# K to gates in a Griffin-style layer: K's second half in another tile order, the first gates' raw weights loaded once, their sums in a pool of their own

## The chip, the cores and the metric

The kernel runs on one core of one Trainium2 chip, in one launch. The metric is the device time of that core in microseconds (us). A time is the median of several executions; beside it stands one profiled execution with its own time.

TensorE (PE) multiplies matrices, VectorE (DVE), ScalarE (ACT) and GpSimd (POOL) work elementwise, SyncE (SP) issues DMAs only. ScalarE issues DMAs too. Each engine runs its own list of instructions in order and waits at semaphores for the others.

## The reference

One layer of a streaming encoder over 1024 tokens, with 1024 channels and 16 heads of 64, in float32:

```python
h = rmsnorm(x, ln1_g[l]) * (1.0 + sc1) + sh1
p = h @ w_in[l]
q, k, v, cb, cc, cx, ga, gb = jnp.split(p, split_at, axis=-1)
q = rmsnorm(q.reshape(b, s_len, SB_HEADS, SB_HEAD_DIM), q_norm_g[l])
k = rmsnorm(k.reshape(b, s_len, SB_HEADS, SB_HEAD_DIM), k_norm_g[l])
v = v.reshape(b, s_len, SB_HEADS, SB_HEAD_DIM)
y_a = stick_breaking_attention(q, k, v)
y_b = cb * causal_dwconv(cc * cx, conv_w[l])
merged = (jax.nn.sigmoid(ga) * (y_a @ w_branch_a[l])
          + jax.nn.sigmoid(gb) * (y_b @ w_branch_b[l]))
x = x + g1 * (merged @ w_out[l])

h = rmsnorm(x, ln2_g[l]) * (1.0 + sc2) + sh2
f = (jax.nn.silu(h @ w_ffn_gate[l]) * (h @ w_ffn_up[l])) @ w_ffn_down[l]
x = x + g2 * f
```

Here the change touches how `k`, and then `q`, `cb`, `cc`, `cx`, `ga` and `gb` are computed.

## The kernel before

**Numbers.** Every product is computed from two parts of each float32 operand, a rounded one (hi) and the rest (lo), as three matmuls: hi·hi, lo·hi and hi·lo. ScalarE makes hi with a copy, VectorE makes lo by a subtraction. A pair hi/lo made from weights is `whi` and `wlo`; `hh[n]` and `hl[n]` (shown as `big`) hold the parts of h, transposed, for token half n and eight chunks of channels.

**Stages.** Normalisation of x; V; K; the "gates" (the other six column sections of `w_in`); attention; branches and output; the FFN. The change is where K ends and the gates begin, at some 100 to 215 us.

**K.** Two column halves (`cc` = 1, 2, loop at L450), each over eight tiles of 128 tokens. A tile is a product of 24 matmuls (`mm_tok`, L308) into a bank `pj`, and then `finish_k` (L395): ScalarE squares (`qsq`, L397), VectorE adds up per head (`qss`, L399), POOL makes the reciprocal root in two steps (`rs_m`, L122, and `rs_r`, L123), VectorE scales (`qn`, L402). What stands behind the `yield`, TensorE's transposes (`tr`, L408), hi and lo (`khl`, L411 on ScalarE and L412 on VectorE) and the two stores to `d_k` (L414, issued by ScalarE), is run two tiles later, from the list `tails`; the last two are run between the first products of the gates. Beside K, a generator (`ml`, `more()`) makes sums of parts of h, which are written to `d_t` on SyncE (L376) and come back as the factors of the gates.

**Gates.** 20 gates of 1024 x 256 weight columns (1024 x 1024 per section, in four): four of q, eight of the convolution, eight of the gates proper. Each gate is a 2 x 2 block product with seven products in place of eight (Winograd's form): p1 to p7, each 12 matmuls (`half_prod`, L131 to L133). The raw weights of a gate are two 512 KB loads (`g_raw`, L478, a ring of two buffers): a11 and a12 in the first, a21 and a22 in the second. POOL makes s3 = a11 − a21, s2 = a22 − s3, s1 = a21 + a22 and s4 = a12 − s2 (`ws`, L136 and L653). `g_split` (L489) splits each, p1 and p2 take the first raw half as it is. The other factor is a part of h (p1, p2, p3) or one of the sums `d_t`: `ft5` with s2 (p6), `ft4` with s1 (p5), `ft6` with s3 (p7), and d_t3 with a22 (p4), which is loaded into `hh[1][:, 0:4]` and `hl[1][:, 0:4]` (L644; K's last tiles read these before). Products are combined into `c` on VectorE; the first `c` is a copy of p1 on ScalarE (L682).

The products p1 and p2 of gates 0 and 1 run ahead (`pre`, L505 to L516), straight behind K, from a raw half each; for their other products both gates load both raw halves (again).

**q.** Each finished quarter of q goes through `put_q`: hi and lo (`gt`, L588 on ScalarE, L589 on VectorE) are stored to `d_q`, then its square (`c`, L590) is split into hi (`gt`, L591) and lo (`gt`, L136, the helper of all VectorE and POOL operations on two tensors), and `sum_q` (L599) adds the squares up with a one-hot matmul `tr<-gt,sel`, some products later (`later`).

**Order.** What runs when on each engine is decided by a scheduler that places instructions by their dependences and expected times, in the order of the program where these don't decide; `tc.high_priority()` moves what is inside ahead of what competes with it, `tc.issue_after` holds something behind a given instruction. Names that end in a number are buffers or versions of a tile.

Of the kernel before, what the change touches and what calls it, by code (L numbers as in the profile page):

```python
# [29 lines left out]
def block_kernel(tc, x, x_t, cols, ada_1, ada_2, ada_row, w_q, w_kv, w_v1, w_cg, w_a, w_b, w_o, w_g, w_u, w_d, out):  # L30
# [8 lines left out]
    def nm(s):  # L39
        uid[0] += 1  # L40
        return f"{s}_{uid[0]}"
# [100 lines left out]
    def ps_pj():  # L142
        return pps.tile([P, 512], F32, tag="pj", bufs=6, name=nm("pj"))
# [301 lines left out]
    def more():  # L445

        with tc.issue_after(ends[0]), tc.issue_after(ends[1]):
            next(ml, None)

    for cc in (1, 2):  # L450
        w = wq[4:] if cc == 1 else [load_w(w_kv[cc, j]) for j in range(4)]
        for i in range(8):
            ps = ps_pj()
            mm_tok(ps, i, w, 0, 8)
            while len(tails) >= 2:
                next(tails.pop(0), None)
            tails.append(finish_k(ps, i, cc - 1))
            next(tails[-1])
            for _ in range(2 if (cc, i) < (1, 4) else 3):
                more()  # L460
            if (cc, i) == (2, 1):
                for _ in ml:
                    pass
                s2b.close()
                sx.close()

    ftx = ExitStack()
    ftp = ftx.enter_context(tc.tile_pool(name="phft", bufs=1, side="right", reuse_waits="tile"))
    ft = {q: ftp.tile([P, 2, 4, 512], F32R, name=f"ft{q}") for q in (5, 4)}
    for q in (5, 4):  # L470
        nc.sync.dma_start(ft[q].bitcast(F32), d_t[q])

    def g_bank():
        return ps_pj()

    def g_raw(src):
        raw = gw.tile([P, 1024], F32, tag="raw", bufs=GR, name=nm("raw"))
        last_raw[0] = nc.sync.dma_start(raw, src)  # L478
        return raw
# [5 lines left out]
    def g_split(src):  # L485
# [4 lines left out]
        tt(nc.vector, lo, src, hi.bitcast(F32), ALU.subtract)  # L490
        return hi, lo

    fac = {0: (hh[0][:, 0:4], hl[0][:, 0:4]), 1: (hh[0][:, 4:8], hl[0][:, 4:8]), 2: (hh[1][:, 4:8], hl[1][:, 4:8])}
    def g_prod(w, q):
        ps = g_bank()
        half_prod(ps, w, *fac[q])
        return ps

    gates = ([(5, j) for j in range(4)] + [(sec, j) for j in range(4) for sec in (1, 2)] +
             [(sec, j) for sec in (4, 3) for j in range(4)])  # L500

    def w_of(sec, m):
        return w_q[m] if sec == 5 else w_cg[sec, m]

    pre = {}  # L505

    def first_two(g):
        sec, j = gates[g]
        raw = g_raw(w_of(sec, j))
        return g_prod(g_split(raw[:, :512]), 0), g_prod(g_split(raw[:, 512:]), 1)  # L510

    for g in range(NG):
        pre[g] = first_two(g)
        if g == 0:
            for tl in tails:
                next(tl, None)  # L516

    def two_raw(g):
        sec, j = gates[g]
        return g_raw(w_of(sec, j)), g_raw(w_of(sec, j + 4))  # L520

    s2.close()
    sw.close()
# [3 lines left out]
    gp = sg_.enter_context(tc.tile_pool(name="phg1", bufs=1, reuse_waits="tile"))  # L527

    split_at.append(gp)
    ft[6] = gp.tile([P, 2, 4, 512], F32R, name="ft6")  # L530
    for q, t in ft.items():
        fac[q] = (t[:, 0], t[:, 1])
    fac[3] = (hh[1][:, 0:4], hl[1][:, 0:4])
# [103 lines left out]
        nc.scalar.dma_start(d_y[m, :, s:s + 512], y)  # L637

    uc = {}
    raws = two_raw(0)  # L640
    pend, pmm, eq = [], [], end_q()
    nc.sync.dma_start(ft[6].bitcast(F32), d_t[6])
    for e in range(2):
        nc.sync.dma_start(fac[3][e].bitcast(F32), d_t[3][:, e])  # L644
    for g, (sec, j) in enumerate(gates):
        raw, raw2 = raws
        p1, p2 = pre[g] if g in pre else (g_prod(g_split(raw[:, :512]), 0), g_prod(g_split(raw[:, 512:]), 1))
        a11, a12, a21, a22 = raw[:, :512], raw[:, 512:], raw2[:, :512], raw2[:, 512:]
        s1, s2_, s3, s4 = (gp.tile([P, 512], F32, tag=f"ws{q}", bufs=1, name=nm("ws")) for q in range(4))
        tt(nc.gpsimd, s3, a11, a21, ALU.subtract)  # L650
        tt(nc.gpsimd, s2_, a22, s3, ALU.subtract)
        tt(nc.gpsimd, s1, a21, a22, ALU.add)
        ws4 = nc.gpsimd.tensor_tensor(out=s4, in0=a12, in1=s2_, op=ALU.subtract)  # L653
        if g + 1 < len(gates):
            raws = two_raw(g + 1)
        c11, c21, c12, c22 = (gp.tile([P, 512], F32, tag=f"c{q}", bufs=2, name=nm("c")) for q in range(4))

        def put(c, m, n):
            if sec == 5:
                pend.append((c, m, n))  # L660
            elif sec > 2:
                nc.scalar.activation(c, c, AF.Sigmoid)
                nc.scalar.dma_start((d_sga, d_sgb)[sec - 3][m, :, n * 512:(n + 1) * 512], c)
            elif sec == 1:
                ccs[m, n] = c
            elif n == 1 and m >= 4:
                ccs["late"] = c
            else:
                put_u(c, m, n)
                if n == 0 and m >= 4:  # L670
                    put_u(ccs["late"], m, 1)

        def later():
            if len(pmm) > 1 or pmm and not pend:
                sum_q(*pmm.pop(0))
            if pend:
                put_q(*pend.pop(0))
            elif g > 3 and not pmm:
# [24 lines left out]
        put(c21, j + 4, 0)  # L703
        if g + 1 == len(gates):
            for _ in eq:
                pass
        for _ in range((5 if sec in (3, 4) else 0) if g + 1 < len(gates) else 50):
            next(ml, None)
    sg_.close()
    ftx.close()  # L710
    split_at[:] = [gw]
# [887 lines left out]
```

## Time and profile before

| | us |
|---|---|
| median of 3 executions | 1842.04 (1841.74 to 1842.79) |
| profiled execution, its own time | 1840.08 |
| its span | 1838.3 |
| mean granted clock of TensorE | 0.998 |

The span is what the page and the views divide; the execution's own time lies 1.8 us above it. Rows of a timeline give start, duration, engine and line, operation, output and inputs (partitions x elements) and, in brackets, how long the engine had been idle and what ended that. A row with x2 or x3 is several in sequence. "SPq" and "ACTq" are DMAs issued by SyncE or ScalarE. TensorE is continuously busy from 66 to 178 us, and the stretch of the change ends at some 215.

### The profile page before, as it was taken

To read this page: it belongs to the slowest core of one execution; us is meant where nothing else is said; L and a number is where in the kernel's file an instruction comes from. 1 tells how busy PE (TensorE), PEld (TensorE's weight loads), DVE (VectorE), ACT (ScalarE), POOL (GpSimd) and SP (SyncE) were. 2 spreads that over 40 slices of the span, in tenths; PEclk is the share of its full clock that TensorE was granted. 3 is DMA by queue.
4 is the path that set the end of the run, shared out by engine and by line. 5 is a ranking of instruction groups with operands and counts; after the bars stand their busy time and mean duration, and the time that the engine had idled before them with its cause. 6 is when DMAs were issued, how large, how long until landed. Compare 5 with 4: busy or idle time off the path is not lost.

```text
span 1838.3 us, 24895 instructions
## 1 busy us (share of the span) xinstructions
PE 1803.6 (98%) x8829; PEld 1501.9 (82%) x8829; DVE 1353.5 (74%) x1949; ACT 792.3 (43%) x1494; POOL 366.4 (20%) x277
## 2 busy tenths in 40 slices
PE   7999999999999999999999999999999999999999
PEld 4787778888889988888888788877888888878887
DVE  7873776779874888888887644589877788644776
ACT  3452553333343656665665311664444344422321
POOL 0043327423240000000000000105544454200000
PEclk9999999999999999999999999999999999999999
DMA  9598452217748566588544636424533344299766
GB/s 395 198 317 303 162 188 76 86 70 260 275 157 265 153 183 180 178 240 278 153 133 141 209 126 209 142 92 161 195 138 147 130 172 170 103 340 334 283 228 221
DMA packets 147267, 358.01 MB, mean 195 GB/s; under 512 B 15480, under 2 KB 44480, under 8 KB 144968
## 3 DMA queue, kind: packets, MB, share of 16 engines
q1 hardware_dynamic: 101816, 289.12, 46.3%
q10 hardware_dynamic: 44320, 63.64, 9.9%
q0 software_dynamic: 1008, 3.67, 0.5%
q8 instruction: 70, 1.15, 0.3%
q14 instruction: 53, 0.43, 0.1%
HBM read 245.74 MB, written 110.66 MB: 194 GB/s over the span
## 4 chain that ended last, share of the span: by engine, by line
PE 76%; DVE 11%; DMA 6%; issue 3%; ACT 3%; POOL 0%; ACTq 0%; SPq 0%; DVEq 0%; POOLq 0%
PE e L131 6%; PE e L132 6%; PE e L133 6%; PE pj L131 5%; PE pj L133 5%; PE pj L132 5%; PE pj L308 5%; PE pj L892 4%; PE pj L893 4%; PE pj L894 4%; PE e L1427 4%; PE e L1426 4%; PE e L1428 4%; PE tr L819 3%; PE o L835 2%
## 5 line engine op out<-in xcount | busy, mean ns | idle before, releaser
L804 DVE TENSOR_TENSOR_SCAN pt<-pt,mk 128x128 f32<-128x128 f32 (+7 forms) x128 | 172.1, 1350 | 48.8 <-ACT pt L800 48.6
L800 ACT ACTIVATE pt<-z,rq 128x512 f32<-128x512 f32 (+3 forms) x192 | 107.3, 580 | 88.9 <-PE z L799 57.4
L131 PE MATMUL e<-big,whi 128*128 128x512 f32 x352 | 137.7, 391 | 1.9 <-ACT c L1326 1.9
L133 PE MATMUL e<-big,wlo 128*128 128x512 f32 x352 | 137.7, 391 | 0.0
L132 PE MATMUL e<-big,whi 128*128 128x512 f32 x352 | 137.6, 391 | 0.0
L136 DVE TENSOR_TENSOR c<-e,c 128x512 f32<-128x512 f32 x138 | 93.0, 687 | 56.0 <-PE e L133 55.0
L122 POOL TENSOR_SCALAR rs_m<-ss 128x1 f32<-128x1 f32 x8 | 1.5, 192 | 651.8 <-ACT xn L1229 651.8
L131 PE MATMUL pj<-big,whi 128*128 128x512 f32 x320 | 125.1, 391 | 0.5 <-DVE c L136 0.4
L132 PE MATMUL pj<-big,whi 128*128 128x512 f32 x320 | 124.7, 390 | 0.0
L133 PE MATMUL pj<-big,wlo 128*128 128x512 f32 x320 | 124.4, 390 | 0.0
L1426 PE MATMUL e<-whi,f 128*128 128x512 f32 (+1 forms) x319 | 121.7, 382 | 1.6 <-DMA f<-d_f 1.6
L1427 PE MATMUL e<-wlo,f 128*128 128x512 f32 (+1 forms) x319 | 121.8, 382 | 0.0
L1428 PE MATMUL e<-whi,f 128*128 128x512 f32 (+1 forms) x319 | 121.6, 382 | 0.0
L136 DVE TENSOR_TENSOR c<-pj,c 128x512 f32<-128x512 f32 x140 | 93.2, 682 | 27.3 <-PE pj L133 26.4
L136 DVE TENSOR_TENSOR wlo<-raw,whi 128x512 fp32r<-128x512 f32 x116 | 88.1, 763 | 34.2 <-ACT whi L489 34.1
L308 PE MATMUL pj<-whi,big 128*128 128x512 f32 x352 | 109.4, 396 | 3.7 <-ACT big L291 3.6
L489 ACT ACTIVATE whi<-raw 128x512 fp32r<-128x512 f32 x116 | 72.7, 631 | 89.1 <-PE pj L132 38.8
L823 DVE TENSOR_TENSOR atl<-tr,ath 128x512 fp32r<-128x512 f32 (+1 forms) x192 | 99.6, 548 | 14.4 <-ACT ath L822 12.6
L136 POOL TENSOR_TENSOR ws<-raw,raw 128x512 f32<-128x512 f32 x40 | 55.4, 1384 | 273.6 <-DMA raw<-w_cg 165.2
L822 ACT ACTIVATE ath<-tr 128x512 fp32r<-128x512 f32 (+1 forms) x192 | 86.9, 490 | 44.8 <-PE o L834 26.0
L132 PE MATMUL e<-rl,whi 128*128 128x512 f32 x264 | 103.6, 392 | 2.5 <-DVE rl L136 2.5
L892 PE MATMUL pj<-big,whi 128*128 128x512 f32 x256 | 103.9, 406 | 0.0
(258 smaller groups left out, 5015.9 us busy)
## 6 DMA issues: line engine op xcount, KB each, us to landing
f<-d_f SPq DMA_DIRECT2D x77, 512.0 KB, 3.6
d_f<-fs SPq DMA_DIRECT2D x70, 512.0 KB, 3.2
raw<-w_cg SPq DMA_DIRECT2D x40, 512.0 KB, 4.4
raw<-w_u SPq DMA_DIRECT2D x26, 512.0 KB, 3.2
raw<-w_g SPq DMA_DIRECT2D x25, 512.0 KB, 3.4
ad<-ada ACTq DMA_DIRECT2D x19, 512.0 KB, 5.0
ada<-ada SPq DMA_DIRECT2D x8, 1024.0 KB, 9.6
d_t<-ts SPq DMA_DIRECT2D x16, 512.0 KB, 4.0
```

Of the source, the lines that this page charges most:

```text
L131: nc.tensor.matmul(ps, wh[:, k, :], fh[:, k, :], start=(k == 0), stop=False)
L132: nc.tensor.matmul(ps, wh[:, k, :], fl[:, k, :], start=False, stop=False)
L133: nc.tensor.matmul(ps, wl[:, k, :], fh[:, k, :], start=False, stop=(k == 3))
L136: eng.tensor_tensor(out=out, in0=a, in1=b, op=op)
L308: nc.tensor.matmul(ps, a, b, start=(k == 0 and q == 0), stop=(k == KT - 1 and q == 2))
L800: nc.scalar.activation(pt[:, off + s0:off + s0 + m], z[:, :m], AF.Sigmoid, scale=rq[:, 1, i, h:h + 1])
L804: nc.vector.tensor_tensor_scan(out=pt[:, rev], data0=pt[:, rev], data1=mk[:, rev], initial=1.0, op0=ALU.mult, op1=ALU.max)
L823: nc.vector.tensor_tensor(out=tl[:, :nb, c0:c0 + P], in0=src, in1=th[:, :nb, c0:c0 + P].bitcast(F32), op=ALU.subtract)
L892: nc.tensor.matmul(ps, wh, rh_, start=(k == 0), stop=False)
L1426: nc.tensor.matmul(o, sh, w[0][:, c], start=(j == 0), stop=False)
L1427: nc.tensor.matmul(o, sh, w[1][:, c], start=False, stop=False)
L1428: nc.tensor.matmul(o, sl, w[0][:, c], start=False, stop=(j == NJ - 1))
```

## The change

- The second half of K (`cc` = 2) takes its tiles in the order 4, 5, 6, 7, 0, 1, 2, 3. After four of them, no matmul of K reads `hh[1]` any more, and d_t3 is loaded over it there.
- Gate 1's first raw half is loaded for `pre` first and split within K's loop; then both raw halves of gate 0 are loaded, and kept for all of gate 0's products. Gate 1's first half is still loaded twice. Products p1 and p2 of gate 1 now run ahead of gate 0's.
- The sums `ws` have a pool of their own (`gp2`), so that they need not wait for the pools of the K stage to be given back. For gate 0, s3, s2 and the split of s2 (`w6`) are under high priority; the split of s2 is written ahead of the other products for all gates.
- ft6 is loaded under high priority, behind the last raw load.
- For gate 0, p3 is computed ahead of p7.
- The stores of K: in both kernels all 32 are issued by ScalarE; none stands on SyncE's queue.

```diff
-    for cc in (1, 2):
-        w = wq[4:] if cc == 1 else [load_w(w_kv[cc, j]) for j in range(4)]
-        for i in range(8):
...
+    for cc in (1, 2):
+        w = wq[4:] if cc == 1 else [load_w(w_kv[cc, j]) for j in range(4)]
+        for i_, i in enumerate(range(8) if cc == 1 else (4, 5, 6, 7, 0, 1, 2, 3)):
+            if (cc, i_) == (2,4):
+                for e in range(2):
+                    ld = nc.sync.dma_start((hh, hl)[e][1][:, 0:4].bitcast(F32), d_t[3][:, e])
+            if (cc, i_) == (2,3):
+                raw1 = g_raw(w_of(*gates[1]))
+                pre_w = [(g_split(raw1[:, :512]), g_split(raw1[:, 512:]))]
+                raws = two_raw(0)
             ps = ps_pj()
             mm_tok(ps, i, w, 0, 8)
...
-    pre = {}
-
-    def first_two(g):
-        sec, j = gates[g]
-        raw = g_raw(w_of(sec, j))
-        return g_prod(g_split(raw[:, :512]), 0), g_prod(g_split(raw[:, 512:]), 1)
-
-    for g in range(NG):
-        pre[g] = first_two(g)
-        if g == 0:
-            for tl in tails:
-                next(tl, None)
...
+    pre_w.append((g_split(raws[0][:, :512]), g_split(raws[0][:, 512:])))
+    pre = {1: tuple(g_prod(pre_w[0][q], q) for q in range(2))}
+    for tl in tails:
+        next(tl, None)
+    pre[0] = tuple(g_prod(pre_w[1][q], q) for q in range(2))
...
     split_at.append(gp)
+    for t_ in ("whi", "wlo"):
+        gp.tile([P, 512], F32R, tag=t_, bufs=GS2, name=nm(t_))
     ft[6] = gp.tile([P, 2, 4, 512], F32R, name="ft6")
+    sg2 = ExitStack()
+    gp2 = sg2.enter_context(tc.tile_pool(name="phg2", bufs=1, reuse_waits="tile"))
...
-    raws = two_raw(0)
     pend, pmm, eq = [], [], end_q()
-    nc.sync.dma_start(ft[6].bitcast(F32), d_t[6])
-    for e in range(2):
-        nc.sync.dma_start(fac[3][e].bitcast(F32), d_t[3][:, e])
+    with tc.high_priority(), tc.issue_after(last_raw[0].ins):
+        nc.sync.dma_start(ft[6].bitcast(F32), d_t[6])
...
-        s1, s2_, s3, s4 = (gp.tile([P, 512], F32, tag=f"ws{q}", bufs=1, name=nm("ws")) for q in range(4))
-        tt(nc.gpsimd, s3, a11, a21, ALU.subtract)
-        tt(nc.gpsimd, s2_, a22, s3, ALU.subtract)
+        s1, s2_, s3, s4 = (gp2.tile([P, 512], F32, tag=f"ws{q}", bufs=1, name=nm("ws")) for q in range(4))
+        with tc.high_priority() if g == 0 else ExitStack():
+            tt(nc.gpsimd, s3, a11, a21, ALU.subtract)
+            tt(nc.gpsimd, s2_, a22, s3, ALU.subtract)
+            w6 = g_split(s2_)
         tt(nc.gpsimd, s1, a21, a22, ALU.add)
...
-        p6 = g_prod(g_split(s2_), 5)
+        p6 = g_prod(w6, 5)
...
+        p3 = g_prod(g_split(s4), 2) if g == 0 else None
         p7 = g_prod(g_split(s3), 6)
...
-        p3 = g_prod(g_split(s4), 2)
+        p3 = p3 or g_prod(g_split(s4), 2)
```

SyncE's queue, from the last two stores of factors to the first raw loads of the gates, before:

```order
49 L376 DMA d_t_85<-ts_1132 256x1x512
50 L471 DMA ft_1414<-d_t_86 128x4096
51 L471 DMA ft_1413<-d_t_85 128x4096
52 L644 DMA big_149<-d_t_84 128x2048
53 L644 DMA big_218<-d_t_84 128x2048
54 L478 DMA raw_1517<-w_q 128x1024
55 L478 DMA raw_1519<-w_q 128x1024
56 L642 DMA ft_1514<-d_t_83 128x4096
57 L478 DMA raw_1532<-w_q 128x1024
58 L478 DMA raw_1534<-w_q 128x1024
```

and now:

```order
49 L376 DMA d_t_85<-ts_1132 256x1x512
50 L452 DMA raw_1197<-w_q 128x1024
51 L505 DMA ft_1430<-d_t_86 128x4096
52 L482 DMA big_149<-d_t_84 128x2048
53 L482 DMA big_218<-d_t_84 128x2048
54 L505 DMA ft_1429<-d_t_85 128x4096
55 L452 DMA raw_1539<-w_q 128x1024
56 L646 DMA ft_1520<-d_t_83 128x4096
57 L452 DMA raw_1541<-w_q 128x1024
```

Gate 0's second raw half (now raw_1197, before raw_1519) stands ahead of the factors ft4 and ft5 instead of behind them and big; its first half is loaded once, further up. The first half for gate 1 (raw_1539) is ahead of ft6, the second behind it.

POOL's list, at the end of K, before (`rs_m`, `rs_r`: one pair for each K tile; `ws`: s3, s1, s2, s4 of gate 0):

```order
41 L122 TENSOR_SCALAR rs_m_1360<-qss_1357 128x8
42 L123 TENSOR_TENSOR rs_r_1361<-rs_m_1360,nhalf 128x8
43 L122 TENSOR_SCALAR rs_m_1405<-qss_1402 128x8
44 L123 TENSOR_TENSOR rs_r_1406<-rs_m_1405,nhalf 128x8
45 L136 TENSOR_TENSOR ws_1526<-raw_1517,raw_1519 128x512
46 L136 TENSOR_TENSOR ws_1524<-raw_1519 128x512
47 L136 TENSOR_TENSOR ws_1525<-raw_1519,ws_1526 128x512
48 L653 TENSOR_TENSOR ws_1527<-raw_1517,ws_1525 128x512
```

and now, within K:

```order
35 L136 TENSOR_TENSOR ws_1529<-raw_1195,raw_1197 128x512
36 L136 TENSOR_TENSOR ws_1527<-raw_1197 128x512
37 L122 TENSOR_SCALAR rs_m_1239<-qss_1236 128x8
38 L136 TENSOR_TENSOR ws_1528<-raw_1197,ws_1529 128x512
39 L123 TENSOR_TENSOR rs_r_1240<-rs_m_1239,nhalf 128x8
40 L657 TENSOR_TENSOR ws_1530<-raw_1195,ws_1528 128x512
41 L122 TENSOR_SCALAR rs_m_1286<-qss_1283 128x8
42 L123 TENSOR_TENSOR rs_r_1287<-rs_m_1286,nhalf 128x8
```

Gate 0's four sums moved from behind K's last pair to around the pair of an earlier tile: four more pairs of K follow behind row 40. The third sum, s2, stands between that tile's rs_m and rs_r.

ScalarE's list where K ends, before (`khl`: the last two transposed tiles of K; `c`: copies of p1 of gates 0 and 1; `whi` from `ws`: splits of gate 0's sums):

```order
146 L411 ACTIVATE khl_1458<-tr_1453,cst 128x512
147 L414 DMA d_k_66<-khl_1395 128x4x128
148 L414 DMA d_k_65<-khl_1458 128x4x128
149 L414 DMA d_k_66<-khl_1458 128x4x128
150 L411 ACTIVATE khl_1468<-tr_1463,cst 128x512
151 L414 DMA d_k_65<-khl_1468 128x4x128
152 L414 DMA d_k_66<-khl_1468 128x4x128
153 L682 ACTIVATE c_1536<-pj_1423 128x512
154 L682 ACTIVATE c_1676<-pj_1479 128x512
155 L489 ACTIVATE whi_1569<-ws_1524 128x512
156 L489 ACTIVATE whi_1541<-ws_1525 128x512
```

and now:

```order
147 L463 ACTIVATE whi_1572<-ws_1527 128x512
148 L463 ACTIVATE whi_1607<-ws_1529 128x512
149 L411 ACTIVATE khl_1472<-tr_1467,cst 128x512
150 L414 DMA d_k_65<-khl_1472 128x4x128
151 L414 DMA d_k_66<-khl_1472 128x4x128
152 L411 ACTIVATE khl_1482<-tr_1477,cst 128x512
153 L414 DMA d_k_65<-khl_1482 128x4x128
154 L414 DMA d_k_66<-khl_1482 128x4x128
155 L463 ACTIVATE whi_1533<-ws_1528 128x512
156 L686 ACTIVATE c_1543<-pj_1487 128x512
```

Two splits (of s1 and s3) moved ahead of K's last two tiles, and the split of s2 (whi_1541 before, whi_1533 now) stands straight behind the last store, ahead of the copies. On TensorE the last of K's transposes (four rows, `tr<-dm,qn`) had 8 matmuls of p1 and p2 between it and the first matmul of p6, and has 16 now; the second last had 40, and has 24.

More of the change, by code (lines that the diff above doesn't have):

```diff
@@ L448, in more @@
             next(ml, None)
-    for cc in (1, 2):
-        w = wq[4:] if cc == 1 else [load_w(w_kv[cc, j]) for j in range(4)]
-        for i in range(8):
[L453 to L474, printed above, removed]
     def g_raw(src):
@@ L491, in g_split, with w_of, two_raw, g_bank @@
         return hi, lo
+    gates = ([(5, j) for j in range(4)] + [(sec, j) for j in range(4) for sec in (1, 2)] +
+             [(sec, j) for sec in (4, 3) for j in range(4)])
+    def w_of(sec, m):
+        return w_q[m] if sec == 5 else w_cg[sec, m]
+    def two_raw(g):
+        sec, j = gates[g]
+        return g_raw(w_of(sec, j)), g_raw(w_of(sec, j + 4))
+    for cc in (1, 2):
[8 more added lines that the diff above has]
+                raws = two_raw(0)
+            ps = ps_pj()
+            mm_tok(ps, i, w, 0, 8)
+            while len(tails) >= 2:
+                next(tails.pop(0), None)
+            tails.append(finish_k(ps, i, cc - 1))
+            next(tails[-1])
+            for _ in range(2 if (cc, i_) < (1, 4) else 3):
+                more()
+            if (cc, i_) == (2, 1):
+                for _ in ml:
+                    pass
+                s2b.close()
+                sx.close()
+    ftx = ExitStack()
+    ftp = ftx.enter_context(tc.tile_pool(name="phft", bufs=1, side="right", reuse_waits="tile"))
+    ft = {q: ftp.tile([P, 2, 4, 512], F32R, name=f"ft{q}") for q in (5, 4)}
+    for q in (5, 4):
+        nc.sync.dma_start(ft[q].bitcast(F32), d_t[q])
+    def g_bank():
+        return ps_pj()
     fac = {0: (hh[0][:, 0:4], hl[0][:, 0:4]), 1: (hh[0][:, 4:8], hl[0][:, 4:8]), 2: (hh[1][:, 4:8], hl[1][:, 4:8])}
@@ L497, in g_prod @@
         return ps
[L499 to L503, printed above, removed]
-    pre = {}
-    def first_two(g):
-        sec, j = gates[g]
-        raw = g_raw(w_of(sec, j))
-        return g_prod(g_split(raw[:, :512]), 0), g_prod(g_split(raw[:, 512:]), 1)
-    for g in range(NG):
-        pre[g] = first_two(g)
-        if g == 0:
-            for tl in tails:
-                next(tl, None)
-    def two_raw(g):
-        sec, j = gates[g]
-        return g_raw(w_of(sec, j)), g_raw(w_of(sec, j + 4))
+    pre_w.append((g_split(raws[0][:, :512]), g_split(raws[0][:, 512:])))
[3 more added lines that the diff above has]
+    pre[0] = tuple(g_prod(pre_w[1][q], q) for q in range(2))
     s2.close()
@@ L708, in block_kernel @@
             next(ml, None)
+    sg2.close()
     sg_.close()
```

## The prediction

> **What bounds the kernel now.** I read the page first, for the engine that sets the end, and its chain of waits.
>
> ```profile
> PE 1803.6 (98%) x8829; PEld 1501.9 (82%) x8829; DVE 1353.5 (74%) x1949; ACT 792.3 (43%) x1494; POOL 366.4 (20%) x277
> PE 76%; DVE 11%; DMA 6%; issue 3%; ACT 3%; POOL 0%; ACTq 0%; SPq 0%; DVEq 0%; POOLq 0%
> ```
>
> TensorE is busy for 98% of the span, and the matmuls stay the same in number and shape. So the change can give only what TensorE waits near the junction of the K stage and the gates, and it can take only by making TensorE wait there. The view of waits over 60 to 215 us says how much that is (columns: total, times, longest).
>
> ```profile
> PE pj L131 <- ACT whi L489: 2.3, 1, 2.3
> PE tr L599 <- DVE gt L136: 1.5, 1, 1.5
> PE tr L599 <- ACT gt L591: 0.3, 1, 0.3
> ```
>
> Three TensorE waits, 4.1 us idle. A matmul's end is modelled, so I price them from start to start, in TensorE's timeline.
>
> ```profile
> 177.38 0.39 PE L132 MATMUL pj<-big,whi 128*128 128x512 f32 x1
> 177.61 0.40 PE L133 MATMUL pj<-big,wlo 128*128 128x512 f32 x1
> 180.27 0.50 PE L131 MATMUL pj<-ft,whi 128*128 128x512 f32 x1 [2.27 <-ACT whi L489]
> 180.61 0.40 PE L132 MATMUL pj<-ft,whi 128*128 128x512 f32 x1
> ...
> 198.33 0.39 PE L132 MATMUL pj<-ft,whi 128*128 128x512 f32 x1
> 199.03 0.40 PE L599 MATMUL tr<-gt,sel 128*16 128x512 f32 x1 [0.31 <-ACT gt L591]
> ...
> 203.65 0.40 PE L132 MATMUL pj<-big,whi 128*128 128x512 f32 x1
> 205.56 0.40 PE L599 MATMUL tr<-gt,sel 128*16 128x512 f32 x1 [1.51 <-DVE gt L136]
> ```
>
> One matmul follows the other after 0.23 (177.38 to 177.61). The first wait costs 2.66 − 0.23 = 2.43, and the slower next step 0.34 − 0.23 = 0.11; the second 0.70 − 0.23 = 0.47; the third 1.91 − 0.23 = 1.68. Together 4.69 us. That is all that can be won here.
>
> The timelines of the other engines show why the first wait is there.
>
> ```profile
> 163.73 1.89 DVE L136 TENSOR_TENSOR wlo<-raw,whi 128x512 fp32r<-128x512 f32 x3
> 165.04 3.60 SPq L478 DMA_DIRECT2D raw<-w_q  x2
> 175.16 1.28 POOL L136 TENSOR_TENSOR ws<-raw,raw 128x512 f32<-128x512 f32 x1 [6.13 <-DMA raw<-w_q]
> 177.66 1.27 POOL L136 TENSOR_TENSOR ws<-raw,ws 128x512 f32<-128x512 f32 x1
> 176.18 0.69 ACT L411 ACTIVATE khl<-tr,cst 128x512 fp32r<-128x512 f32 x1 [7.05 <-PE tr L408]
> 176.90 1.15 ACTq L414 DMA_DIRECT2D d_k<-khl  x2
> 179.07 1.67 ACT L489 ACTIVATE whi<-ws 128x512 fp32r<-128x512 f32 x3
> ```
>
> Both raw buffers hold the first gates' weights until VectorE splits them at 163.7. Only then can SyncE load gate 0's pair again (165.0), which lands at about 175.1. POOL's third sum (s2 = a22 − s3) ends at 178.9, ScalarE splits it, and TensorE, through with its previous block at 177.61 + 0.23 = 177.84, starts at 180.27.
>
> **The change, part by part.** All times below are on the clock of this profile.
>
> *Raw weights once, sums early.* One 512 KB load goes away; it lies under other work, so by itself it is worth nothing. Gate 1's raw half is split as soon as ScalarE and VectorE can (about 134) and its buffer takes gate 0's second half at about 136, ahead of the factor loads on SyncE's queue. The nearest landings, from SyncE's timeline, the chain of waits, the view of the K stores' line and the transfers of 130 to 200 us:
>
> ```profile
> 136.44 1.59 SPq L471 DMA_DIRECT2D ft<-d_t  x2
> 182.66 4.18 DMA raw<-w_q
> L414 ACTq DMA_DIRECT2D d_k<-khl x32: 366/366/3173, 102.9 to 177.7; - x32
> DMA to landing us min/median/max: 2.2/4.5/14.7
> ft<-d_t SPq DMA_DIRECT2D x3, 2048.0 KB, 8.3
> ```
>
> A raw load took 4.18 at 182.66; the longest landing of any K store, beside the factor loads, 14.7. So this raw lands between 140.3 and 150.8; ahead of the factors on its own queue, I take the low end, 140.3. POOL then does four sums of 1.28 among the normalisation of one tile of K's second half. In the timelines of POOL, VectorE and TensorE that tile and its transposes, two tiles later, stand so:
>
> ```profile
> 143.36 0.20 POOL L122 TENSOR_SCALAR rs_m<-qss 128x8 f32<-128x8 f32 x1 [4.01 <-DVE qss L399]
> 145.31 0.69 DVE L402 TENSOR_TENSOR qn<-pj,rs_r 128x512 f32<-128x512 f32 x1 [1.38 <-POOL rs_r L123]
> 153.63 0.60 PE L408 MATMUL tr<-dm,qn 128*128 128x128 f32 x4
> ```
>
> Two sums end at 142.9, before rs_m is due (143.36); the third stands between rs_m and rs_r and delays qn by 1.3, while the transposes that read qn come 153.63 − 146.00 = 7.6 later. Cost 0; without that cover it would be the 1.3. At 150.8 it is a rival (below). The third sum is then there 30 us before it is wanted.
>
> *ScalarE at the junction.* Before, the last transposes are followed by 8 matmuls of the block, now by 16: they come 8 × 0.227 = 1.8 earlier, so the last khl starts at 176.18 − 1.82 = 174.4. Behind it on ScalarE stand its two K stores and then the split of s2. By the rows above: 174.4 + 0.72 (khl until the first issue) + 1.15 (two issues) = 176.2, and 0.6 for the split (three took 1.67) gives 176.8, against TensorE's need at 177.84: margin 1.0. The splits of s1 and s3, four rows earlier, have several us. So the first wait goes: **−2.54**. Below, the margin of 1.0 is what the four K store issues from 172 on may cost more than usual. Their price has two ends: the row says 0.366 for most of the 32 and 3.17 for the worst. The slow pairs, in ScalarE's timeline, with ft6's issue on SyncE and the row of 166 to 182 us in the view by windows (busy time of each engine, granted clock, DMA share, GB/s):
>
> ```profile
> 143.16 3.97 ACTq L414 DMA_DIRECT2D d_k<-khl  x2
> 149.10 2.92 ACTq L414 DMA_DIRECT2D d_k<-khl  x2
> 173.32 0.33 SPq L642 DMA_DIRECT2D ft<-d_t  x1
> 166.00:182.00 16.00, 13.73 (x64) 10.97 (x64) 6.33 (x12) 5.94 (x11) 6.88 (x6) 1.00 1.03 372
> ```
>
> A pair took 1.15 at 176.90, 2.92 and 3.97 at 149 and 143. They ran while two factor loads of 2 MB (136.44) were in flight; the pair at 176.90 ran beside one (173.32), with the engines just as full (DMA share 1.03 in 166 to 182). After the change there is one again: ft6, which I place at about 169, and ft4, ft5 and big are issued before 150. So I take 1.15, the nearer row, and keep 3.97 for the range.
>
> The Trainium skill, "DMA: Bandwidth & Descriptors", section "Queues, rings and completion order", speaks against this cover: SyncE and ScalarE each have a ring on the same 16 DMA engines, and each engine takes turns between the rings packet by packet. By that ft6 slows the last K stores wherever it is queued, and they would at worst land with it, so that the sum would move towards R2; the landing of 14.7 agrees with such sharing, and the issue of 1.15 at 176.90 does not ask for more than that.
>
> *Factor loads and order of products.* big (d_t3) goes from its issue behind K to about 145; ft6 is issued some 4 earlier. A block of 12 matmuls takes 12 × 0.227 = 2.72. ft5 is needed at 177.84, big at 177.84 + 2 × 2.72 = 183.3, and ft6, behind p3 now, at 186.0, 17 us after its issue; the median landing of the three 2 MB factors is 8.3. Cost 0; without the cover, ft6 would have to be 8.7 later than that before it costs anything.
>
> *Gate 0's and gate 1's ends (the second and third wait).* These are VectorE and ScalarE running late behind the sums of the next gate, in the timelines of POOL and VectorE.
>
> ```profile
> 187.00 1.29 POOL L136 TENSOR_TENSOR ws<-raw,raw 128x512 f32<-128x512 f32 x1 [6.72 <-DMA raw<-w_q]
> 199.17 1.24 DVE L136 TENSOR_TENSOR gt<-c,gt 128x512 fp32r<-128x512 f32 x1
> 200.33 1.78 DVE L136 TENSOR_TENSOR wlo<-raw,whi 128x512 fp32r<-128x512 f32 x1
> 202.04 1.78 DVE L589 SCALAR_TENSOR_TENSOR gt<-c,cst,gt 128x512 fp32r<-128x512 f32 x1
> 203.75 0.68 DVE L136 TENSOR_TENSOR c<-pj,c 128x512 f32<-128x512 f32 x1
> 204.35 1.16 DVE L136 TENSOR_TENSOR gt<-c,gt 128x512 fp32r<-128x512 f32 x1
> 201.52 1.76 POOL L136 TENSOR_TENSOR ws<-raw,ws 128x512 f32<-128x512 f32 x1
> ```
>
> Beside POOL's sums VectorE's operations with two inputs in SBUF take 1.2 to 1.8 where c<-pj,c, one of whose inputs is a TensorE bank, takes 0.68. After the change gate 0's four splits are no longer in VectorE's way behind 180, and its gt rows move up before gate 1's splits. I walked the new order with these durations: gate 1's second raw, issued when a22 has been split (179.2), lands 4.18 later at 183.4; POOL's sums end by 188.7; the split of gate 1's s2 stands on ScalarE behind a gt that waits for p7 and ends at 190.9, wanted at 191.9; gate 0's last gt is ready at 200.5 (wanted 203.5), gate 1's at 208 and 211.8 (wanted 209 and 212.8). Each is in time, by 1 us at three places: the worst case is that these waits stay (R1), the best that both vanish (−2.15). As three margins of 1 us will hardly all hold to the end, I give back the smaller of the two waits, 0.47, and take **−1.68**.
>
> The Trainium skill's "GPSIMD Engine Reference", section "Specifications", names the same sharing: the SBUF interfaces of GpSimd are shared with VectorE, with contention for VectorE operations with two SBUF inputs. The rows agree (1.78 against 0.68). Taken by itself it speaks against this gain, since gate 1's sums still meet VectorE from 183 to 189: by it the time would be R1's.
>
> *K's tile order.* The same 8 tiles; the stores go to other addresses of d_k. Cost 0. Elsewhere the only reordering that touches a wait is in the FFN:
>
> ```profile
> L131 PE MATMUL e<-big,whi 128*128 128x512 f32 x352 | 137.7, 391 | 1.9 <-ACT c L1326 1.9
> ```
>
> One VectorE split less stands ahead there, which is 0.63 of the 1.9 at most (three splits took 1.89 at 163.73); I take 0 and keep −0.6 for the low end.
>
> *Sum:* 2.54 + 1.68 = 4.22, with all waits 4.69. The profiled execution took 1840.08 with a span of 1838.3; it becomes 1835.9. It lies 1.96 under the median of the runs, 1842.04, which becomes **1837.8**.
>
> **The rivals.**
>
> R1, *the first wait goes, the others stay or move.* VectorE is as late at the ends of gates 0 and 1, since POOL still slows it to 1.78. For: three margins of 1.0. Against: four splits fewer behind 180. Gain 2.54: 1839.5.
>
> R2, *slower: the last K stores starve behind ft6.* They sit on ScalarE ahead of the split of s2, and ft6 now starts before them. For: pairs of 2.92 and 3.97 beside factor loads. Against: 1.15 at 176.90 beside ft6. If three of the four issues take 3.17 instead of 0.37, the split is 8.4 late, less the margin of 1.0: 7.4 in place of the 2.54 of before; the later stages follow, and gate 0's first gt on ScalarE, whose buffer a K store must have left, is held too, so that the later waits stay: 1842.04 + 7.4 − 2.54 = 1846.9. It costs more than the whole gain from 4.69 + 1.0 = 5.7 us of delay on. A single slow issue (2.8 − 1.0 = 1.8) gives 1839.6.
>
> R3, *gate 0's second raw lands late.* At 150.8 two sums hold rs_m until 153.4; qn starts 1.95 after rs_m (143.36 to 145.31) and 1.28 for the sum between, and ends at 157.3, so that the transposes of 153.63 wait 3.7: 1841.5. Against: it is ahead of the factors on its queue.
>
> R4, *part of the change isn't there.* No K store stands on SyncE's queue in the new order; all 32 are on ScalarE's. So the last of the change's four parts gives nothing, and what it would have removed (two issues ahead of the split, 1.15) is no term above. That is settled by the order, and lies in all cases.
>
> **How the numbers follow.** Forecast 0.52, R1 0.21 (with a single slow issue), R3 0.08, R2 0.11, and 0.08 for a wait that I don't see, of 2 to 4 us: 1840 to 1842. The predicted time is the forecast's, 1837.8. Its own range runs from 1836.7 (4.69 and the FFN's 0.6) to 1838.6; R1 and the single issue reach 1839.6, R3 1841.5. The range is 1836.7 to 1841.6, with R2 outside. 0.2%, about what a measurement of this kernel can tell from no change, is 3.7 us: faster means under 1838.4, which needs the first wait and most of the third. Faster 0.52, within 0.2% 0.36 (R1, R3, the unseen wait), slower 0.12.
>
> **What would show it.** In the new profile: POOL's four sums of gate 0 between 140 and 148; no TensorE wait for a ScalarE whi at about 178; no wait of over 0.5 for tr of gates 0 and 1 up to 215; the four last K store issues under 0.8 each. Wrong: TensorE waiting for whi of s2 behind a K store (R2), for qn in K's second half (R3), or for gt with VectorE at 1.8 an operation (R1); or waits at places that were not touched.

## The result, and the profile after

| | before | after |
|---|---|---|
| median of 10 executions, us | 1842.55 (1841.13 to 1848.23) | 1837.20 (1834.27 to 1842.99) |
| ratio to before, 95% interval | | 0.9970 (0.9957 to 0.9982) |
| profiled execution, us | 1840.08 | 1842.99 |
| its span, us | 1838.3 | 1841.2 |

The changed kernel is faster by 0.30% (0.18 to 0.43%), 5.4 us by the medians. The prediction said 1837.8. The two profiled executions contradict that at first sight: the one of after is the longest of its ten, and the one of before lies under all ten timed ones. So I read what the change did at the place of the change, and the rest of the span by itself.

TensorE's timeline of after, around the two waits that the view of waits shows between 66 and 215 us:

```profile
159.24 0.39 PE L308 MATMUL pj<-whi,big 128*128 128x512 f32 x1
161.45 0.63 PE L408 MATMUL tr<-dm,qn 128*128 128x128 f32 x4 [1.82 <-DVE qn L402]
...
179.48 0.39 PE L133 MATMUL pj<-big,wlo 128*128 128x512 f32 x1
180.16 0.50 PE L131 MATMUL pj<-ft,whi 128*128 128x512 f32 x1 [0.29 <-ACT whi L463]
180.50 0.39 PE L132 MATMUL pj<-ft,whi 128*128 128x512 f32 x1
```

The wait of 2.3 for whi is down to 0.3, the waits for gt behind it are gone, and a new one of 1.82 stands in K, where before had none. Its cause, in the timelines of SyncE, ScalarE, POOL and VectorE of after:

```profile
135.59 0.34 SPq L452 DMA_DIRECT2D raw<-w_q  x1
136.30 0.34 SPq L505 DMA_DIRECT2D ft<-d_t  x1
138.91 0.80 SPq L482 DMA_DIRECT2D big<-d_t  x2
139.76 0.44 SPq L505 DMA_DIRECT2D ft<-d_t  x1
143.07 14.14 ACTq L414 DMA_DIRECT2D d_k<-khl  x2
157.25 0.60 ACT L397 ACTIVATE qsq<-pj 128x512 f32<-128x512 f32 x1 [14.22 <-DMA d_k<-khl]
158.66 0.20 POOL L122 TENSOR_SCALAR rs_m<-qss 128x8 f32<-128x8 f32 x1 [10.96 <-DVE qss L399]
160.62 0.69 DVE L402 TENSOR_TENSOR qn<-pj,rs_r 128x512 f32<-128x512 f32 x1 [1.39 <-POOL rs_r L123]
```

SyncE puts 0.5 + 2 + 2 + 2 = 6.5 MB in line within 5 us. The next pair of K stores, behind it on ScalarE's queue, takes 14.14 us to issue, where the pair at the same place took 3.97 before and a pair with no load in line takes 1.2. ScalarE's square of the next tile stands behind that issue, and through qss, rs_m, rs_r and qn the transposes, due at 159.47, are 2.0 late. The transfers by queue in 143 to 156 us (packets, MB, share of the engines' time; q1 is SyncE's queue, q10 ScalarE's), before and then after:

```profile
q1 hardware_dynamic: 162, 2.13, 45.3%
q10 hardware_dynamic: 3139, 1.56, 40.1%
```

```profile
q1 hardware_dynamic: 474, 4.64, 84.8%
q10 hardware_dynamic: 1266, 0.63, 16.2%
```

In the same 13 us the K stores move 0.63 MB instead of 1.56, while SyncE's loads move 4.64 instead of 2.13. The Trainium skill, "DMA: Bandwidth & Descriptors", section "Queues, rings and completion order", has both queues share the 16 engines by turns of packets. The shares agree in that the stores keep getting turns while the larger packets take the time (1266 packets in 16.2% of it, 474 in 84.8%); they do not show one packet for one, as the profile counts packets. That the issue holds ScalarE meanwhile is told by the rows of 14.14 and 14.22.

The early sums are where they were expected, in POOL's timeline of after:

```profile
140.26 1.29 POOL L136 TENSOR_TENSOR ws<-raw,raw 128x512 f32<-128x512 f32 x1 [1.00 <-DMA raw<-w_q]
143.27 0.20 POOL L122 TENSOR_SCALAR rs_m<-qss 128x8 f32<-128x8 f32 x1 [0.47 <-DVE qss L399]
143.54 1.29 POOL L136 TENSOR_TENSOR ws<-raw,ws 128x512 f32<-128x512 f32 x1
```

To compare executions, I take the 864th matmul recorded on TensorE in each; it starts at 215.18 in the profile of before. (The changed kernel places a few of the `tr<-gt,sel` rows otherwise, so there it is a neighbouring row, but as much work lies ahead of it.) After starts it at 213.13, 2.05 earlier: 2.0 lost at 161, 2.0 won at 180, 0.5 and 1.7 won at 199 and 206, and 0.3 lost at 194.5, where gate 1's first p6 matmuls come 0.38 and 0.34 apart in place of 0.23. From there to the end of the span, before takes 1623.1 and after 1628.1 us, on code that the change hardly touches.

### The profile page after: what moved, and what is told of

Read it like the earlier page. It is cut to its first block, busy times and chain, and to the rows that moved or that the text cites. A ratio compares the mean times of both kernels' runs of the same rounds, so it can differ in the third digit from the quotient of the medians.

```text
span 1841.2 us, 24891 instructions
## 1 busy us (share of the span) xinstructions
PE 1803.7 (98%) x8829; PEld 1501.9 (82%) x8829; DVE 1353.7 (74%) x1949; ACT 789.9 (43%) x1494; POOL 367.6 (20%) x277
## 3 DMA queue, kind: packets, MB, share of 16 engines
q8 instruction: 70, 1.15, 0.3%
## 4 chain that ended last, share of the span: by engine, by line
PE 72%; DVE 11%; DMA 9%; issue 3%; ACT 3%; POOL 1%; ACTq 0%; SPq 0%; DVEq 0%; POOLq 0%
PE e L131 6%; PE e L133 6%; PE e L132 6%; PE pj L131 5%; PE pj L133 5%; PE pj L132 5%; PE e L1432 4%; PE e L1433 4%; PE e L1434 4%; PE pj L308 4%; PE pj L898 3%; PE pj L899 3%; PE pj L900 3%; PE tr L825 2%; PE o L841 1%
```

## The experiments

Twelve runs. "At 215" is the start of that 864th matmul against 215.18. after_again, ft5_held, k_order and stores_sync ran on one chip, the other eight on another; so medians are best compared by their ratios to the kernel before, which ran beside each.

| run | at 215 | from there to the end | median (95% interval of the ratio to before) |
|---|---|---|---|
| before, four executions | 0, +0.9, +2.0, +3.1 | 1623.1, 1627.4, 1621.7, 1625.6 | |
| after, on record | −2.1 | 1628.1 | 1837.20 (0.9957 to 0.9982) |
| after_again | −2.1 | 1627.5 | 1839.61 (0.9965 to 0.9984) |
| after_third | −2.3 | 1624.0 | 1839.04 (0.9954 to 0.9979) |
| stores_sync | −2.3 | 1623.2 | 1838.26 (0.9959 to 0.9980) |
| k_order | −2.5 | 1622.4 | 1838.34 (0.9949 to 0.9977) |
| ft5_held | −3.7 | 1623.7 | 1837.42 (0.9940 to 0.9973) |
| held_sync | −4.5 | 1626.6 | 1837.09 (0.9933 to 0.9967) |
| held_sync_again | −4.7 | 1624.5 | 1837.41 (0.9946 to 0.9977) |
| sums_in_gp | +2.6 | 1625.6 | 1844.14 (0.9978 to 1.0002) |
| raw_reload | +5.9 | 1624.3 | 1845.83 (0.9986 to 1.0013) |

**after_again** and **after_third**: the changed kernel, no edit.

> The changed kernel once more, unaltered, for a profile of another execution. The profiled execution on record (1842.99, the longest of ten) lost 2.0 us in K: two K store issues held ScalarE for 14.1 us at 143 while four loads (6.5 MB) were queued, so that TensorE waited 1.8 for qn at 161. Theory: this hold is a matter of each execution, so the profile here has TensorE wait for qn between 0 and 2.5 us, no wait of over 0.5 for gt (tr) up to 215, and a median of 1836 to 1838.5 (4 to 6 us under before). Rival: the two executions profiled are typical and the gain on record came by chance from runs of before: median 1840 to 1843.

> The changed kernel beside held_sync_again on one chip. Theory: at 215 us it stands 2.0 to 2.2 ahead of the first profile of before, with the wait for qn of 1.8 at 161; median 3 to 6 us under before. Rival (the hold of K's stores is not in every execution): no wait at 161 and 4 or more ahead at 215.

The hold of ScalarE comes in every execution: the pair at 143.1 took 14.17 us in after_again and 13.81 in after_third, and TensorE waited 1.86 and 1.50 for qn. At 215 us the three executions are within 0.3 of each other. The rival of the first fell, since 1839.6 and 1839.0 stand 4.2 and 5.7 under the medians of before beside them (1839.6 lies above the range that was expected, too), and so did that of the second.

**ft5_held**: one more condition on the load of ft5.

```diff
-    for q in (5, 4):
-        nc.sync.dma_start(ft[q].bitcast(F32), d_t[q])
+    with tc.issue_after(qns[13].ins):
+        nc.vector.memset(ft[5].bitcast(F32)[:, 0, 0, 0:2], 0.0)
+    nc.sync.dma_start(ft[5].bitcast(F32), d_t[5])
+    nc.sync.dma_start(ft[4].bitcast(F32), d_t[4])
```

Left out here: `qns` collects the qn operations of K's tiles.

> The load of ft5 (2 MB) is held until K's sixth tile of the second half has its qn (about 157), by a two-element memset of ft5 on VectorE that the load overwrites. Theory: K's store issues on ScalarE starve because raw, ft4, big and ft5 are queued together at 136 to 140; with 4.5 MB at once the longest issue of a pair falls from 14 us to at most 6, the wait for qn is gone, and the time is 0.5 to 2 us below after_again. Rival one: the long issue is chance and comes in some executions of either; times within 0.5 us. Rival two: ft5 is late at 178 or the stores of 160 to 175 now starve beside it: TensorE waits for ft5 or whi at 178, 1 us or more slower than after_again.

ScalarE's and TensorE's timelines of ft5_held:

```profile
143.10 4.37 ACTq L414 DMA_DIRECT2D d_k<-khl  x2
151.30 0.93 ACTq L414 DMA_DIRECT2D d_k<-khl  x2
192.82 0.50 PE L131 MATMUL pj<-ft,whi 128*128 128x512 f32 x1 [0.39 <-ACT whi L463]
```

With 4.5 MB in line the pair takes 4.4 instead of 14.1, the K stores move 1.58 MB in 143 to 156 us, about as before, and TensorE has no wait for qn. At 215 us it is 1.4 to 1.7 ahead of the changed kernel, and its median is 2.2 under after_again's (0.5 to 2 was expected); the intervals overlap. So the theory holds, and both rivals fall. What is left is one wait of 0.39 for the whi of gate 1's s2 at 192.8.

**k_order**: K's second half in the old order, big loaded behind K.

```diff
-        for i_, i in enumerate(range(8) if cc == 1 else (4, 5, 6, 7, 0, 1, 2, 3)):
+        for i_, i in enumerate(range(8) if cc == 1 else range(8)):
-            if (cc, i_) == (2,4):
-                for e in range(2):
-                    ld = nc.sync.dma_start((hh, hl)[e][1][:, 0:4].bitcast(F32), d_t[3][:, e])
...
+    for e in range(2):
+        nc.sync.dma_start((hh, hl)[e][1][:, 0:4].bitcast(F32), d_t[3][:, e])
```

> K's second half in the order 0 to 7 again, with the loads of d_t3 (big) behind it, so that they start at about 163 instead of 139; all else as in the changed kernel. Theory: big is first read by p4 of gate 0 at about 189, so the tile order is worth nothing, and 2 MB fewer in the bunch at 136 to 156 make K's store issues shorter (longest pair under 6 us): 0 to 2 us below after_again. Rival: big and ft6 together behind 163 make the last K stores or ft6 (needed at 186) late: TensorE waits 1 to 4 us at 178 to 190, and the time goes up by as much.

The theory holds in K, and the rival's wait comes behind it. ScalarE's and TensorE's timelines of k_order:

```profile
143.02 6.46 ACTq L414 DMA_DIRECT2D d_k<-khl  x2
174.94 4.35 ACTq L414 DMA_DIRECT2D d_k<-khl  x2
180.02 0.50 PE L131 MATMUL pj<-ft,whi 128*128 128x512 f32 x1 [2.16 <-ACT whi L463]
```

Without big among the loads in line the pair at 143 takes 6.5 (under 6 was expected) and costs TensorE nothing. But big (162.6) and ft6 (171.5) now run beside the last K stores: their last pair takes 4.35, and the split of s2, right behind it on ScalarE, makes TensorE wait 2.2 at 178. That is the prediction's rival R2 in a small size. The time does not go up with it, as the rival had it: the median is 1.3 under after_again's, and 0.2 to 0.4 are won at 215 us. So the tile order is worth the wait at 178, and pays about as much for it at 161.

**stores_sync**: the stores of K's last two tiles on SyncE's queue, the part of the change that the prediction's R4 found missing.

```diff
+    kq = [nc.scalar]
...
-            nc.scalar.dma_start(d_k[e][4 * ch:4 * ch + 4, :, i * P:(i + 1) * P].rearrange("j p t -> p j t"),
+            kq[0].dma_start(d_k[e][4 * ch:4 * ch + 4, :, i * P:(i + 1) * P].rearrange("j p t -> p j t"),
...
+    kq[0] = nc.sync
     for tl in tails:
         next(tl, None)
```

> The four stores of K's last two tiles go to SyncE's queue, where they stand ahead of ft6 and of gate 1's second raw (the part of the change's name that its code does not hold). Theory: they cost ScalarE 1.15 us a pair and it has about 1 us to spare, so at most 0.5 us is to be won, and ft6 goes from about 170 to about 176, lands at 184 to 186 against a need at 186: between 0.5 us less and 1.5 us more than after_again. Rival: the issues on ScalarE are what bounds the junction: split of s2 2 us earlier, 1 to 2 us below after_again.

The wait of 0.1 to 0.3 at 180 is gone, ft6 (issued at 178.9) is in time, and the wait for qn stays (1.71). At 215 us it is as far as the changed kernel: with K late by 2 us, the junction had little to win. Its median is 1.4 under after_again's, which lies in the rival's range, but the intervals overlap and nothing at the junction answers to it.

**held_sync** and **held_sync_again**: both edits.

> Both at once: ft5 held until about 157, and the four stores of K's last two tiles on SyncE's queue ahead of ft6. Theory: with ft5 held, the last pair's issues (2.28 beside ft6) are what makes gate 1's second raw late (a wait of 0.4 for whi at 193); with the stores ahead of ft6 they go away, TensorE has no wait from 66 to 215 us, is 4.3 to 4.7 ahead of the profile of before at 215, and the time is 0 to 1 us under ft5_held. Rival: ft6, issued at about 177, lands after 186: a wait of 0.5 to 3 us for it, and as much slower than ft5_held.

> ft5 held and the last four stores on SyncE's queue, beside the changed kernel on one chip. Theory: 4.4 to 4.6 ahead at 215 us, that is 2.3 to 2.5 more than the changed kernel, and a median 1.5 to 3.5 us under it. Rival: what is won at the junction is lost behind it, in waits at 451 to 1270 us: the medians lie within 1 us.

TensorE has no wait between 66 and 215 us in either execution, and stands 4.5 and 4.7 ahead of before's first profile; the sum of its three waits there was 4.69. That is 2.2 to 2.6 ahead of the changed kernel. In the times the two are not told apart: 1837.4 against 1839.0 side by side, with intervals of 0.9946 to 0.9977 and 0.9954 to 0.9979.

**sums_in_gp**: the sums in the pool of the gates, as before.

```diff
-        s1, s2_, s3, s4 = (gp2.tile([P, 512], F32, tag=f"ws{q}", bufs=1, name=nm("ws")) for q in range(4))
+        s1, s2_, s3, s4 = (gp.tile([P, 512], F32, tag=f"ws{q}", bufs=1, name=nm("ws")) for q in range(4))
```

> Gate 0's sums back in the pool of the gates, whose memory K's weights hold until 166: POOL makes them behind K's last normalisation, from about 169 to 174, not at 140 to 148; the order of TensorE, VectorE and ScalarE is unchanged. Theory of the prediction's term (early sums take the wait at 178 away): the split of s1 stands ahead of K's last khl on ScalarE and gets its sum only at about 172, so that khl, stores and the split of s2 come later, and a wait of 0.5 to 2.5 us at 178 is back: 0.5 to 2.5 us slower than after_again. Rival: the raw weights being there early is enough, the sums are in time at 174, and the time is that of after_again within 0.5.

POOL makes the sums from 173.2 on, and the wait at 178 is back; TensorE's timeline of sums_in_gp:

```profile
162.15 0.63 PE L408 MATMUL tr<-dm,qn 128*128 128x128 f32 x4 [2.40 <-DVE qn L402]
183.94 0.50 PE L131 MATMUL pj<-ft,whi 128*128 128x512 f32 x1 [1.71 <-ACT whi L463]
```

The ratio to before is 0.999 against 0.9967 to 0.9974 of the changed kernel. The theory's wait came, and the rival fell: having the raw weights early is not enough. Its size did not hold: the median lies 4.5 over after_again's, where 0.5 to 2.5 was expected, and at 215 us this execution is 4.6 behind after. Of these, 1.4 are the wait at 184 and 0.8 come behind it (a wait of 0.64 for gt at 210.9 among them). The other 2.4 arise in K, where the wait for qn is longer than after's and the granted clock is half for 3.4 us behind it; no run shows that the late sums cause this.

**raw_reload**: gate 0's raw halves loaded again for its sums.

```diff
-                raws = two_raw(0)
+                raw0 = g_raw(w_of(*gates[0]))
...
+    raws = two_raw(0)
     pend, pmm, eq = [], [], end_q()
```

> Gate 0's raw halves are loaded again for its sums, as before, instead of being kept; all else as in the changed kernel. Theory: the second of them must wait until the weights for p1 and p2 are split (about 168 to 170), lands at 174 to 178, and s2 is ready at 179 to 182: the wait of TensorE at 178 is back with 2 to 5 us, and the time is 2 to 5 us over after_again. Rival: the gain came from the order of the products and the splits: the time stays within 1 us of after_again.

The pair is issued from 172 on (before: from 165), POOL's first sum waits for it until 176.0, and the waits are back. TensorE's timeline of raw_reload:

```profile
161.73 0.63 PE L408 MATMUL tr<-dm,qn 128*128 128x128 f32 x4 [1.88 <-DVE qn L402]
183.85 0.50 PE L131 MATMUL pj<-ft,whi 128*128 128x512 f32 x1 [2.12 <-ACT whi L463]
198.96 0.50 PE L133 MATMUL pj<-ft,wlo 128*128 128x512 f32 x1 [0.27 <-DVE wlo L136]
209.85 0.40 PE L603 MATMUL tr<-gt,sel 128*16 128x512 f32 x1 [2.15 <-DVE gt L136]
```

Nothing is left of the gain (0.9986 to 1.0013). The theory's wait holds, at its lower end. The +5.9 at 215 us is more than that wait: behind the first and the last of these four the clock is half for 3.4 us, some 1.6 us each.

**before_again**, **before_third**, **before_fourth**: the kernel before, no edit.

> The kernel before once more, unaltered, for a second profiled execution. Ten to 29 timed executions lie at 1841.1 to 1850.8 and the profile on record, 1840.08, lies under all of them. Theory: the junction is the same in each execution (waits of 2.3 for whi at 180, 0.3 and 1.5 for gt behind it) and what makes executions longer lies elsewhere. Rival: the junction's own waits differ between executions by 1 us or more, and the profile on record showed them small.

> A third profiled execution of the kernel before. So far two of before stand at 0 and 0.9 us behind the first at 215 us, and two of the changed kernel 2.1 ahead of it, while the medians differ by 4 to 5. Theory: the junction gives 2 to 3 us and the rest, 215 us to the end, differs from execution to execution by up to 5 us in both kernels, at the same few places (451, 514, 1028, 1231 and 1267 us): here 0 to 1 behind at 215, 0 to 6 more at the end. Rival: before's junction loses 2 us more in its usual execution than in the two profiled ones: 2 or more behind at 215.

> A fourth profiled execution of the kernel before, with the same two theories: 0 to 1 us behind the first at 215 us and 0 to 6 more at the end, or 2 and more behind at 215.

All four start p6 at 180.2 to 180.3, after a wait of 2.27 to 2.41. Behind it they part. By the theories the junction is the same each time, 0 to 1 behind the first profile at 215 us: before_again (+0.9) just fits, before_third (+2.0) lies at the border of the rival, and before_fourth (+3.1) is the rival's. TensorE's waits of before_again and, under it, of before_third, where the first profile waits 0.31 at 199.03 and not at all behind 205.56:

```profile
199.88 0.40 PE L599 MATMUL tr<-gt,sel 128*16 128x512 f32 x1 [1.25 <-ACT gt L591]
```

```profile
210.68 0.40 PE L599 MATMUL tr<-gt,sel 128*16 128x512 f32 x1 [1.90 <-ACT gt L591]
```

The first of these makes the +0.9 of before_again. before_third and before_fourth lose 1.4 and 1.6 in the 5 us behind the start of p6. before_third wins that back, since it has no wait at 205, and its +2.0 is the wait at 210.68; why that wait is there stays open. The view by windows of before_fourth, and under it the first of these rows in the first profile (behind POOL's busy time stand the granted clock, the DMA share and GB/s):

```profile
180.00:184.00 4.00, 3.81 (x10) 2.99 (x11) 2.91 (x5) 1.69 (x4) 0.00 (x0) 0.58 0.96 338
208.00:212.00 4.00, 4.00 (x12) 3.05 (x11) 4.00 (x8) 3.66 (x7) 0.00 (x0) 0.58 0.77 276
```

```profile
180.00:184.00 4.00, 3.73 (x16) 3.10 (x17) 3.23 (x5) 1.78 (x4) 0.28 (x1) 1.00 0.99 354
```

TensorE's timeline of before_fourth behind the wait:

```profile
180.84 0.63 PE L131 MATMUL pj<-ft,whi 128*128 128x512 f32 x1
181.26 0.63 PE L132 MATMUL pj<-ft,whi 128*128 128x512 f32 x1
181.69 0.63 PE L133 MATMUL pj<-ft,wlo 128*128 128x512 f32 x1
```

A mean of 0.58 over 4 us is half the clock for 3.4 us; matmuls come every 0.43 instead of 0.23. before_fourth has it a second time, behind the wait of 1.93 at 207, and the two, 1.6 each, make its +3.1. The first profile, on which the prediction was made, had neither. The mean of the four at 215 is +1.5, of the three of after −2.2: 3.6 us apart.

## Why the prediction was right, and where it was not

**The time and the direction** held: 1837.8 was forecast in a range of 1836.7 to 1841.6, and the median is 1837.2. The sum behind it did not hold as written.

**The early sums** came as worked out: the raw half landed by 140.26 (140.3 was taken), and POOL's sums ran from 140 to 148. That the wait at 178 hangs on them is shown from two sides: without their own pool, or with the raw weights loaded again, waits of 1.7 and 2.1 are back.

**The first wait, −2.54**: measured −1.9 to −2.2 in three executions. The last pair of stores took 2.23 to 2.54 where 1.15 was taken, beside ft6, so that 0.1 to 0.3 of the wait is left. The sign "under 0.8 each" thus failed for this pair.

**The second and third wait, −1.68**: both went, −0.5 and −1.7, so R1 did not come. One of the three margins of 1 us failed by a little: the split of gate 1's s2 came late (ended 194.46 in after, with K 2 us late), which costs 0.1 to 0.4 in the three executions and shows as the wait of 0.39 in ft5_held. That is what the 0.47 was given back for. The 0.6 of the low end was not won: the wait in the FFN is 2.0 in after, 1.9 before.

**"Factor loads and order of products … Cost 0"** is the step that failed. The prediction moved big forward to about 145 (it is issued at 138.91), beside ft4 and ft5. It saw that the pairs of 2.92 and 3.97 had run beside two factor loads, but asked what a slow pair would do only for the four issues from 172 on. In K, where three factor loads and a raw half now stand together, the pair took 13.8 to 14.2 and cost 1.7 to 2.0 us. R2's mechanism, the store issue that starves, came true in the place of R3, the late normalisation in K. Holding ft5 back (4.4 us for the pair, no wait) shows it, and so does moving big back (6.5, no wait). The prediction also had big needed at 183.3, by p3; its first reader is p4, at about 189 (p3 reads the other half of that buffer). So its early load bought no time by itself and only kept it away from the last K stores (k_order).

**What was not in the sum**: how much dearer before's junction is in other executions than in the profile that was priced. Against that profile the gain is −2.0 − 2.2 + 0.3 + 2.0 in after, and 2.1 to 2.3 in the three executions, about half of the 4.2 that was forecast. Against the mean of the four executions of before it is 3.6, as three of them lose 0.9 to 3.1 more: by a longer wait for gt, by a new one, and by half the clock for 3.4 us behind waits of about 2 us. That the median came out so near to 1837.8 is therefore luck: the 2.0 lost in K, the 1.5 by which before's junction is dearer on the mean, and a rest that no run places.

**Open**: the medians of before and after differ by 4.2 to 5.7 in the three comparisons, and 3.6 is shown at 215 us, from four and three executions. The interval on record (0.18 to 0.43%, 3.3 to 7.9 us) holds 3.6. The stretch behind 215 us varies from 1621.7 to 1628.1 over all kernels, without order; whether the change also gives 1 to 2 us there, no run shows.

**R4** is settled: the stores on SyncE's queue are worth nothing beside the changed kernel, since K is late there anyway, and 0.8 to 0.9 at 215 us once ft5 is held.

## What to carry to other kernels

A load that is moved forward is paid for by whatever issues DMAs beside it: add up the bytes in line at that moment, and look for the engine that will sit in its own issue (here ScalarE, 14 us behind 6.5 MB) with work behind it that others need. Price a wait of TensorE on more than one execution, since the clock may fall behind it. When the effect is smaller than the difference between one execution and the next, compare not the spans but the start of the same instruction just behind the change.

## What the runs showed of the hardware

The pair of K store issues at 143 us holds ScalarE the longer, the more loads SyncE has issued in the 8 us before it: 3.97 to 4.43 us with 4 MB (before, four executions), 4.36 to 4.52 and 6.46 with 4.5 MB (ft5 held, three executions; k_order), 13.8 to 14.7 with 6.5 MB (the other six executions). A pair with no load under way takes 1.2, the last one at 177, beside ft6, 1.15 to 2.5. From 4.5 to 6.5 MB it grows by two to three times.

A wait of 2.27 or 2.41 us at 178 was enough for half the clock (0.58 granted in 180 to 184 us) in two of four executions of before, and in the other two it was not. Up to 215 us the same followed waits of 1.88 and 2.15 (raw_reload), 1.93 (before_fourth) and 2.40 (sums_in_gp), but not those of 2.16 (k_order), 2.12 (raw_reload) and 1.82 (after).

The traces tell the two apart. Within one execution the slow stretches last 3.413 us and start on a grid of 3.413 us: the two of before_fourth start 27.31 us apart (eight times 3.413), the two of raw_reload 47.78 (fourteen times). The view by windows of before_fourth, with the granted clock third from the end:

```profile
177.24:180.65 3.41, 1.14 (x5) 0.63 (x5) 1.35 (x5) 2.63 (x6) 2.64 (x3) 1.00 0.97 332
180.65:184.06 3.41, 3.41 (x10) 2.63 (x9) 2.26 (x4) 1.04 (x3) 0.00 (x0) 0.50 0.99 352
207.96:211.37 3.41, 3.41 (x10) 2.64 (x9) 3.41 (x7) 3.08 (x6) 0.00 (x0) 0.50 0.77 274
```

There the whole wait of 2.27 lies in the one cell ahead of the slow one. In the first profile, whose slow stretches at 1230.82 and 1268.37 fix its grid, a border at 179.5 cuts the same wait into 1.5 and 0.8, and nothing follows. Up to 215 us all six slow stretches follow a cell with 1.88 to 2.40 us of one wait in it; no slow stretch follows a cell with 1.77 or less, nor three others with 1.82 to 1.88. So a wait of 2 us halves the clock or not by where it happens to fall on the grid. This is read off the traces; no run moved a wait against the grid. The Trainium skill, "TensorE: Matmul & The Clock Gate", in its part on the HAM clock gate, names a free-running window of about 3.4 us, which agrees with the length of the slow stretch and with the grid. That such a stretch follows a wait shorter than the window is what these runs add.
